# A two-layer decoder trunk on one core: half-size staging tiles, five modulation units on VectorE, their ends spread over steps, running sums seeded by ScalarE

## The chip, the core and the metric

The kernel runs on one core of a Trainium2 chip. The metric is the device time of one execution in microseconds, the median of repeated runs; the profile is one such execution. TensorE (PE, its weight loads shown apart as PEld), VectorE (DVE), ScalarE (ACT), GpSimd (POOL) and the sequencer that issues the weight transfers (SP) work in parallel, each through its own instructions in a fixed order, and wait for each other by semaphores.

## What is computed

Two layers act on x (256 tokens of 2048 features). Layer 0 has MoBA and sliding-window attention, layer 1 forgetting attention and NSA; each is followed by a squared-ReLU MLP with 8192 hidden features. Everything is float32. A vector c modulates every layer, and this modulation is what the change deals with:

```python
cond = jax.nn.silu(c)
for i in range(DEPTH):
    mod = cond @ ada_w[i] + ada_b[i]                 # (2048) @ (2048, 12288)
    sh1, sc1, g1, sh2, sc2, g2 = split(mod, 6)
    h = rms_norm(x, norm_mix_g[i]) * (1.0 + sc1) + sh1
    y = even_mixer(h, ...) if i % 2 == 0 else odd_mixer(h, ...)   # projections, attention, w_out
    x = x + g1 * y
    h = rms_norm(x, norm_mlp_g[i]) * (1.0 + sc2) + sh2
    x = x + g2 * (square(relu(h @ mlp_up[i])) @ mlp_down[i])
return rms_norm(x, final_norm_g)
```

## The kernel before

All weights are streamed once from HBM, some 600 MB. `load` (L299) brings a tile of 512 rows by 512 columns (1 MB, one transfer at L301) into the pool `wst` (four buffers), and splits it for TensorE in two halves of 128x1024: ScalarE writes the rounded part `wh` (L306), VectorE the remainder `wl` (L308). Each product is then three float32r matmuls: wh with the rounded activation, wh with its remainder, wl with the rounded activation. So one full load feeds 48 matmuls of 256 columns, and this step (load, its two conversions, 48 matmuls) is the unit in which the program advances. `kproj` (L361) is a step of a projection whose sums over the input features are made in five groups (the even input projection) or four (half of layer 0's `mlp_up`): after each group the partial sum of a 128x512 tile is kept in SBUF. Of the two tiles of a step, the second (i == 1) is brought back into PSUM by ScalarE ahead of the next group's matmuls (L370, a "seed") and copied out by ScalarE (L390); the first is added by VectorE (L392). `proj` and `down` are steps whose sums stay in PSUM.

The modulation product, 2048 by 12288 for each layer, is cut into units by `ada` (L226). A unit streams its weight columns through the same `wst` pool (L236). With `tensor` set it runs on TensorE (L241): a matmul for each group of 128 input rows into a 32-partition strip of a PSUM bank `row`, four strips at a time. Without it, VectorE multiplies and adds each group of 128 rows into an accumulator `acc` (L245, L248). At its end (L258 to L268) a unit transposes `acc` on TensorE, four transposes to a block of 512 columns, into the one bank `aux`, VectorE reduces the block (L260), and adds the bias. A 1024-column unit has two such blocks, and both use `aux`.

Units wait in a queue. `tick`, called once in a step, adds a rate to a credit and for each whole credit pulls one transfer of the next unit, with the arithmetic that belongs to it; `need` pulls until named units are done. The rates and the tables that say which units run on TensorE stand at the top of the file. Layer 0's (scale, shift) pairs, all of layer 0's gates g1 (four units, all on TensorE), scales sc2 and shifts sh2 (eight units, two on TensorE), gates g2 (four units, one on TensorE), and then layer 1's twelve units of 1024 columns (VectorE) stand in it in this order: 24 units, nine on TensorE.

In order of time the program has these stages: the even input projection and attention; `down` for `even_w_out`; half of layer 0's `mlp_up` in four groups (`up_streamed`, L659); the rest of layer 0's MLP (`mlp`, L523); layer 1's mixer (`odd`); its `down`; layer 1's MLP. Between them stands a norm, in which PE waits for VectorE and ScalarE.

Instructions are issued in an order that the compiler's scheduler makes from the program's; semaphores are set by it too. `causal_head` (L575) scales the probabilities of an attention head; its 256-column part runs on VectorE (L590) with `NORM_A` off.

## Time and profile before

| | |
|---|---|
| median of 3 runs | 2323.24 us (2321.38 to 2324.72) |
| the profiled execution, its own time | 2327.63 us |
| its span, first to last instruction | 2325.8 us |
| mean granted TensorE clock | 0.983 |
| PE busy | 2243.2 us, 96% |
| DVE busy | 1669.5 us, 72% |
| ACT busy | 1114.7 us, 48% |
| HBM read | 594.95 MB, 257 GB/s over the span |

Busy is the time in which an engine has at least one instruction in flight. Matmuls overlap each other, so a row's mean duration of some 280 ns is the latency of one, not its share of the span. The granted clock is that of TensorE, 1.0 being 2.4 GHz and 0.5 being 1.2 GHz. A unit in what follows is a modulation unit.

### The profile page before, as it was taken

What the parts mean: (1) busy time and instruction counts of PE and PEld (TensorE: products, weight loads), DVE (VectorE), ACT (ScalarE), POOL (GpSimd) and SP (SyncE); (2) the same over time, 40 slices, a digit from 0 to 9 for tenths busy, and PEclk for the clock granted to TensorE, in tenths of its full rate; (3) what the DMA queues carried; (4) which work ended last, traced back from release to release, by engine and by line L of the source; (5) the groups of instructions that cost most, each with busy time, mean ns of one, the idle gap of its engine ahead of it and who ended that gap; (6) DMA issues with size and microseconds to landing.
All of it is one profiled execution on the core that took longest, in us unless ns stands there. A gap on an engine that the chain in (4) does not pass through costs nothing.

```text
span 2325.8 us, 44699 instructions
## 1 busy us (share of the span) xinstructions
PE 2243.2 (96%) x18762; PEld 2156.4 (93%) x18762; DVE 1669.5 (72%) x2456; ACT 1114.7 (48%) x1742; POOL 4.6 (0%) x25
## 2 busy tenths in 40 slices
PE   7899999999999999999999999998999999999998
PEld 5799789899999999999999988998999999999998
DVE  3888888797767777787876988888644654655555
ACT  4555753555744344344444555444544543543543
POOL 0000000000000000000000000000000000000000
PEclk9999999999999999999999999999999999999999
DMA  9899688899978778787857877886655656656652
GB/s 308 322 326 357 228 281 319 278 323 316 321 280 290 271 272 305 274 313 267 311 198 244 310 266 245 329 302 230 197 199 188 194 199 190 192 199 192 191 194 95
DMA packets 285819, 599.94 MB, mean 258 GB/s; under 512 B 14290, under 2 KB 23346, under 8 KB 285618
## 3 DMA queue, kind: packets, MB, share of 16 engines
q1 hardware_dynamic: 285072, 596.34, 74.2%
q8 instruction: 147, 2.41, 0.4%
q10 hardware_dynamic: 546, 0.75, 0.1%
q14 instruction: 54, 0.44, 0.1%
HBM read 594.95 MB, written 2.10 MB: 257 GB/s over the span
## 4 chain that ended last, share of the span: by engine, by line
issue 65%; PE 21%; DVE 7%; DMA 5%; ACT 2%; SPq 0%; POOL 0%; POOLq 0%; DVEq 0%; ACTq 0%
PE mm L386 6%; PE mm L320 6%; DMA wa<-in_ada_w_dram 3%; DVE wl L308 3%; DVE acc L248 2%; PE bank L386 1%; PE row L241 1%; PE mm L329 1%; PE mm L330 1%; PE mm L328 1%; DMA w<-in_odd_w_out_dram 1%; PE bank L593 1%; PE bank L556 1%; ACT wh L306 1%; DVE sacc L155 0%
## 5 line engine op out<-in xcount | busy, mean ns | idle before, releaser
L308 DVE TENSOR_TENSOR wl<-w,wh 128x1024 fp32r<-128x1024 f32 x736 | 878.9, 1220 | 415.2 <-ACT wh L306 414.3
L306 ACT ACTIVATE wh<-w 128x1024 fp32r<-128x1024 f32 x736 | 751.6, 1055 | 855.4 <-PE mm L320 673.4
L320 PE MATMUL mm<-hs,wh 128*128 128x256 f32 x5120 | 886.2, 278 | 3.9 <-DVE hs L408 3.0
L320 PEld LDWEIGHTS mm<-hs,wh 128*128 128x128 f32 x5120 | 776.6, 189 | 5.5 <-DVE hs L408 3.2
L320 PE MATMUL mm<-xs,wh 128*128 128x256 f32 (+1 forms) x4128 | 720.4, 279 | 2.4 <-ACT xs L454 2.2
L320 PE MATMUL mm<-hs,wl 128*128 128x256 f32 x2560 | 711.4, 278 | 4.0 <-DVE wl L308 3.8
L320 PEld LDWEIGHTS mm<-xs,wh 128*128 128x128 f32 (+1 forms) x4128 | 627.8, 189 | 5.6 <-ACT xs L454 3.4
L320 PE MATMUL mm<-xs,wl 128*128 128x256 f32 x2064 | 572.8, 279 | 1.7 <-DVE wl L308 1.6
L320 PEld LDWEIGHTS mm<-hs,wl 128*128 128x128 f32 x2560 | 482.8, 189 | 6.3 <-DVE wl L308 6.0
L248 DVE SCALAR_TENSOR_TENSOR acc<-wa,cond,acc 128x1024 f32<-128x1024 f32 (+1 forms) x360 | 389.1, 1081 | 108.3 <-DMA wa<-in_ada_w_dram 104.0
L320 PEld LDWEIGHTS mm<-xs,wl 128*128 128x128 f32 x2064 | 388.2, 188 | 3.3 <-DVE wl L308 2.8
L386 PE MATMUL mm<-xs,wh 128*128 128x256 f32 x1792 | 318.4, 281 | 0.3 <-ACT wh L306 0.3
L386 PEld LDWEIGHTS mm<-xs,wh 128*128 128x128 f32 x1792 | 273.9, 189 | 19.2 <-issue 9.2
L386 PE MATMUL mm<-xs,wl 128*128 128x256 f32 x896 | 249.6, 279 | 3.1 <-DVE wl L308 3.1
L386 PEld LDWEIGHTS mm<-xs,wl 128*128 128x128 f32 x896 | 169.2, 189 | 4.8 <-DVE wl L308 3.7
L390 ACT ACTIVATE u<-mm 128x512 f32<-128x512 f32 x88 | 51.7, 589 | 70.3 <-PE mm L386 69.5
L565 ACT ACTIVATE p<-p,st 128x128 f32<-128x128 f32 (+1 forms) x96 | 40.2, 420 | 29.3 <-DVE st L579 14.7
L536 ACT ACTIVATE t<-mm 128x256 f32<-128x256 f32 x96 | 36.4, 379 | 34.1 <-PE mm L320 24.6
L386 PE MATMUL mm<-wh,xs 128*128 128x256 f32 x256 | 50.0, 290 | 0.9 <-ACT wh L306 0.8
L258 PE MATMUL aux<-cst,acc 128*128 128x128 f32 x192 | 31.5, 285 | 19.6 <-DVE s L260 10.2
L241 PE MATMUL row<-wa,cond 128*32 128x512 f32 x288 | 47.1, 628 | 2.1 <-DMA wa<-in_ada_w_dram 2.1
L151 ACT ACTIVATE t<-xT 128x256 f32<-128x256 f32 x60 | 24.6, 414 | 45.3 <-DVE xT L471 45.3
(214 smaller groups left out, 1458.2 us busy)
## 6 DMA issues: line engine op xcount, KB each, us to landing
wa<-in_ada_w_dram SPq DMA_DIRECT2D x160, 1024.0 KB, 6.2
w<-in_mlp_up_dram SPq DMA_DIRECT2D x128, 1024.0 KB, 5.7
w<-in_mlp_down_dram SPq DMA_DIRECT2D x128, 1024.0 KB, 5.1
w<-in_odd_w_in_dram SPq DMA_DIRECT2D x44, 1024.0 KB, 5.7
wa<-in_ada_w_dram SPq DMA_DIRECT2D x64, 512.0 KB, 5.9
w<-in_even_w_in_dram SPq DMA_DIRECT2D x27, 1024.0 KB, 7.0
w<-in_even_w_out_dram SPq DMA_DIRECT2D x16, 1024.0 KB, 5.3
w<-in_odd_w_out_dram SPq DMA_DIRECT2D x16, 1024.0 KB, 6.5
```

Source lines behind the costliest of these rows:

```text
L151: A.activation(s, xT[:, kt, :], AF.Square)
L241: T.matmul(row[32 * i:32 * i + 32, :], cond[:, k:k + 1].to_broadcast([128, 32]), w[:, i, :], start=t == 0, stop=t == KT // kn - 1, tile_po ...
L248: V.scalar_tensor_tensor(acc, w[:, i, :], cond[:, k:k + 1], acc, op0=ALU.mult, op1=ALU.add)
L258: T.transpose(ps[:, i, :], acc[:, 512 * b + 128 * i:512 * b + 128 * i + 128], ident)
L306: A.activation(wh, w[:, g:g + KS, :], AF.Copy)
L308: V.tensor_tensor(wl, w[:, g:g + KS, :], wh.bitcast(F32), op=ALU.subtract)
L320: T.matmul(P[0:m, 0:S], st[:, c0:c0 + m], mv, start=f and i == 0, stop=e and i == 2)
L328: T.matmul(Ps[j][:, 0:n], hi, wh[:, c0:c0 + n], start=f, stop=False)
L386: T.matmul(Ps[i][:, 256 * h:256 * h + 256], st, mv, start=first and e == 0, stop=last and e == 2, skip_group_check=True)
L390: A.activation(flat[i], P, AF.Copy)
L536: A.activation(r, P[:, 0:S], AF.Relu)
L565: A.activation(p[:, o:o + n], p[:, o:o + n], AF.Exp, bias=m[:, i:i + 1], accum_out=den[:, i:i + 1])
```

## The change

Seven things are changed together.

- `wst` has eight buffers of half the size; `load` issues two transfers of 256 rows by 512 columns instead of one of 512 rows, and a unit's transfer carries half as many rows. `tick` adds twice the rate, so the rows of a unit that go with a step stay as they were at an equal rate.
- Two of the four g1 units, both sh2 units and the g2 unit that ran on TensorE go to VectorE. On VectorE they are joined into 1024-column units: one for the second half of g1, four for (sc2, sh2), two for g2. All of these have 16 transfers, and one multiply-add of 128x1024 goes with each.
- A unit on TensorE takes its four strips in turn over two transfers (two strips for each).
- A unit's end is no longer done at once. `columns` puts its blocks in a queue `late`; a `tick` takes one of them before it pulls, and `need` takes all. The two blocks of a unit use two banks, `aux` and `row`.
- In `kproj` both tiles of a step are seeded and copied out by ScalarE; the addition on VectorE goes.
- `NORM_A` is on. The rate during `down` of `even_w_out` goes from 0.7 to 1.0, and g1 is asked for block by block in that stage rather than ahead of it.
- The compression weights of the odd layer are loaded in halves too.

```diff
-NS = 4
+NS = 8
-R_OUT = 0.7
+R_OUT = 1.0
-NORM_A = False
+NORM_A = True
@@ ada
-            kn = D // cols
+            kn = KS * 512 // cols
...
-                        T.matmul(row[32 * i:32 * i + 32, :], cond[:, k:k + 1].to_broadcast([128, 32]), w[:, i, :], start=t == 0, stop=t == KT // kn - 1,
-                                 tile_position=(0, 32 * i))
+                        q = 32 * (k % 4)
+                        T.matmul(row[q:q + 32, :], cond[:, k:k + 1].to_broadcast([128, 32]), w[:, i, :], start=k < 4, stop=k >= KT - 4,
+                                 tile_position=(0, q))
...
-                    for b in range(n // 4):
-                        ps = aux((128, 4, 128))
...
+                    columns(l, secs, c0, cw, tensor, acc)
...
+        late = deque()
+
+        def columns(l, secs, c0, cw, tensor, acc):
+            red = s32()
+            blocks = cw * len(secs) // 512
+
+            def block(b):
+                ps = psx.tile([128, 4, 128], F32, tag=("aux", "row")[b], name="cps")
+                for i in range(4):
+                    T.transpose(ps[:, i, :], acc[:, 512 * b + 128 * i:512 * b + 128 * i + 128], ident)
+                src = ps.rearrange("p a (j q) -> p a j q", q=32)[:, :, :, 0] if tensor else ps
+                V.tensor_reduce(red[:, 4 * b:4 * b + 4], src, AX.X, ALU.add)
+                if b < blocks - 1:
+                    return
...
+            for b in range(blocks):
+                late.append(lambda b=b: block(b))
@@ tick and need
-            credit[0] += rate[0]
+            if late:
+                late.popleft()()
+            credit[0] += 2 * rate[0]
...
+            while late:
+                late.popleft()()
@@ load
-            w = wst.tile([128, kn, ncol], F32, tag="w", name="w")
-            SP.dma_start(w, W[r0:r0 + 128 * kn, c0:c0 + ncol].rearrange("(k p) n -> p k n", p=128))
             for g in range(0, kn, KS):
+                w = wst.tile([128, KS, ncol], F32, tag="w", name="w")
+                SP.dma_start(w, W[r0 + 128 * g:r0 + 128 * (g + KS), c0:c0 + ncol].rearrange("(k p) n -> p k n", p=128))
...
@@ kproj
-            seeded = [g > 0 and not held and i == 1 for i in range(len(outs))]
+            seeded = g > 0 and not held
...
-                        if g == 0 or held or seeded[i]:
-                            A.activation(flat[i], P, AF.Copy)
-                        else:
-                            V.tensor_tensor(flat[i], P, flat[i], op=ALU.add)
+                        A.activation(flat[i], P, AF.Copy)
@@ the queue of units
+        queue(0, (2,), True, 0, 512)
+        queue(0, (2,), True, 512, 512)
+        queue(0, (2,), False, 1024, 1024)
         for g in range(4):
-            queue(0, (2,), G1_T[g] == "1", 512 * g, 512)
-        for g in range(4):
-            queue(0, (4,), SC2_T[g] == "1", 512 * g, 512)
-            queue(0, (3,), SH2_T[g] == "1", 512 * g, 512)
-        for g in range(4):
-            queue(0, (5,), G2_T[g] == "1", 512 * g, 512)
+            queue(0, (4, 3), False, 512 * g, 512)
+        for c0 in (0, 1024):
+            queue(0, (5,), False, c0, 1024)
```

Two places show what this does to the order of instructions. Rows with an x are repeated instructions; line numbers differ between the two kernels (L258 and L263 are the transposes of a unit's end, L260 and L265 their reductions, L248 and L245 the multiply-adds, L308 and L321 the remainders `wl`).

In `mlp` of layer 0, the TensorE stream of before around the end of a 1024-column unit:

```order
L258 MATMUL aux<-cst,acc 128x128 x4
L320 MATMUL mm<-hs,wh 128x256 x2
L320 MATMUL mm<-hs,wl 128x256
L320 MATMUL mm<-hs,wh 128x256 x2
L320 MATMUL mm<-hs,wl 128x256
L320 MATMUL mm<-hs,wh 128x256 x2
L320 MATMUL mm<-hs,wl 128x256
L320 MATMUL mm<-hs,wh 128x256 x2
L320 MATMUL mm<-hs,wl 128x256
L320 MATMUL mm<-hs,wh 128x256 x2
L320 MATMUL mm<-hs,wl 128x256
L258 MATMUL aux<-cst,acc 128x128 x4
```

The second block's four transposes stand 15 matmuls behind the first's. The same stream of the changed kernel around the first block of such an end:

```order
L333 MATMUL mm<-hs,wh 128x256 x2
L333 MATMUL mm<-hs,wl 128x256
L263 MATMUL cps<-cst,acc 128x128 x4
L333 MATMUL mm<-hs,wh 128x256 x2
L333 MATMUL mm<-hs,wl 128x256
L333 MATMUL mm<-hs,wh 128x256 x2
L333 MATMUL mm<-hs,wl 128x256
```

Here the second block's transposes follow 32 rows (48 matmuls, one step) further on, and they write another bank.

The VectorE stream of before at such an end (`acc` by L245 opens the next unit, `mod` is the finished piece of the modulation):

```order
L245 TENSOR_SCALAR acc<-wa,cond 128x1024
L260 TENSOR_REDUCE s<-aux 128x4
L308 TENSOR_TENSOR wl<-w,wh 128x1024
L260 TENSOR_REDUCE s<-aux 128x4
L308 TENSOR_TENSOR wl<-w,wh 128x1024
L265 TENSOR_TENSOR mod<-s,adab 128x8
```

And of the changed kernel:

```order
L245 SCALAR_TENSOR_TENSOR acc<-wa,cond,acc 128x1024
L321 TENSOR_TENSOR wl<-w,wh 128x1024
L265 TENSOR_REDUCE s<-cps 128x4
L321 TENSOR_TENSOR wl<-w,wh 128x1024
L245 SCALAR_TENSOR_TENSOR acc<-wa,cond,acc 128x1024 x2
L321 TENSOR_TENSOR wl<-w,wh 128x1024
L265 TENSOR_REDUCE s<-cps 128x4
L321 TENSOR_TENSOR wl<-w,wh 128x1024
L272 TENSOR_TENSOR mod<-s,adab 128x8
```

The two reductions had one instruction between them and now have four, multiply-adds of the next unit among them; and that next unit's first `acc` no longer stands ahead of the first reduction.

In the streamed half of `mlp_up`, the ScalarE stream of the changed kernel (L383 is the seed, L402 the copy out, L319 the rounded part `wh`), where before each step had one seed and one copy out:

```order
L402 ACTIVATE u<-mm 128x512
L383 ACTIVATE mm<-u 128x512
L402 ACTIVATE u<-mm 128x512
L319 ACTIVATE wh<-w 128x1024
L383 ACTIVATE mm<-u 128x512
L319 ACTIVATE wh<-w 128x1024
```

These six rows are one step: two copies out, two seeds and two conversions.

## Rows read from the trace of the kernel before

**Rows 1.** The page: busy time by engine, and DMA in 40 slices.
```profile
PE 2243.2 (96%) x18762; PEld 2156.4 (93%) x18762; DVE 1669.5 (72%) x2456; ACT 1114.7 (48%) x1742; POOL 4.6 (0%) x25
...
DMA  9899688899978778787857877886655656656652
```

**Rows 2.** Stretches: us, busy us of each engine (instructions), granted clock, DMA share, GB/s.
```profile
30.00:205.00 175.00, 160.78 (x1297) 154.02 (x1298) 142.81 (x158) 91.46 (x126) 0.00 (x0) 0.95 0.93 328
...
297.00:402.00 105.00, 104.95 (x892) 100.34 (x887) 90.41 (x156) 50.17 (x80) 0.00 (x0) 1.00 0.87 306
402.00:610.00 208.00, 198.20 (x1662) 184.52 (x1661) 161.72 (x230) 125.18 (x190) 0.69 (x1) 0.98 0.90 307
610.00:1173.00 563.00, 544.65 (x4684) 538.96 (x4684) 429.22 (x504) 237.73 (x312) 0.00 (x0) 0.98 0.81 289
...
1740.00:1798.00 58.00, 58.00 (x514) 58.00 (x514) 24.52 (x21) 25.70 (x33) 0.00 (x0) 1.00 0.61 194
```

**Rows 3.** Groups by shape: count, busy us, mean ns, idle before, its releasers.
```profile
L241 PE MATMUL row<-wa,cond 128*32 128x512 f32 x288 | 47.1, 628 | 2.1 <-DMA wa<-in_ada_w_dram 2.1
...
L258 PE MATMUL aux<-cst,acc 128*128 128x128 f32 x192 | 31.5, 285 | 19.6 <-DVE s L260 10.2 <-DVE acc L248 8.1 <-ACT acc L254 1.1
```

**Rows 4.** TensorE's modulation matmuls alone, by stretch: us, PE, PEld, ACT busy, clock, DMA.
```profile
404.00:418.00 14.00, 4.04 (x16) 0.49 (x16) 0.00 (x0) 0.81 0.95 330
...
580.00:616.00 36.00, 4.26 (x32) 0.63 (x32) 0.59 (x1) 1.00 0.90 312
```

**Rows 5.** Order of time at a unit's end: start us, us, engine, operation, idle before.
```profile
840.25 0.28 PE L320 MATMUL mm<-xs,wl 128*128 128x256 f32 x1
843.37 0.75 DVE L245 TENSOR_SCALAR acc<-wa,cond 128x1024 f32<-128x1024 f32 x1 [4.10 <-DMA wa<-in_ada_w_dram]
844.03 0.68 DVE L260 TENSOR_REDUCE s<-aux 128x4 f32<-128x512 f32 x1
...
844.77 1.11 PE L258 MATMUL aux<-cst,acc 128*128 128x128 f32 x4 [4.24 <-DVE s L260]
```

**Rows 6.** Stretches: behind that end, at two norms, and with the most traffic.
```profile
844.00:852.00 8.00, 7.23 (x44) 7.23 (x45) 5.02 (x8) 0.65 (x1) 0.00 (x0) 0.65 0.43 130
404.00:418.00 14.00, 10.26 (x60) 5.96 (x59) 11.17 (x22) 5.12 (x10) 0.69 (x1) 0.81 0.95 330
...
180.00:190.00 10.00, 10.00 (x90) 10.00 (x89) 9.74 (x9) 4.20 (x7) 0.00 (x0) 1.00 1.03 383
```

**Rows 7.** Groups by shape on DVE and ACT.
```profile
L308 DVE TENSOR_TENSOR wl<-w,wh 128x1024 fp32r<-128x1024 f32 x736 | 878.9, 1220 | 415.2 <-ACT wh L306 414.3
L306 ACT ACTIVATE wh<-w 128x1024 fp32r<-128x1024 f32 x736 | 751.6, 1055 | 855.4 <-PE mm L320 673.4 <-PE mm L330 34.2 <-PE mm L386 33.9
...
L248 DVE SCALAR_TENSOR_TENSOR acc<-wa,cond,acc 128x1024 f32<-128x1024 f32 x225 | 288.1, 1280 | 89.5 <-DMA wa<-in_ada_w_dram 87.3
...
L248 DVE SCALAR_TENSOR_TENSOR acc<-wa,cond,acc 128x512 f32<-128x512 f32 x135 | 101.0, 748 | 18.8 <-DMA wa<-in_ada_w_dram 16.7
L390 ACT ACTIVATE u<-mm 128x512 f32<-128x512 f32 x88 | 51.7, 589 | 70.3 <-PE mm L386 69.5
...
L392 DVE TENSOR_TENSOR u<-mm,u 128x512 f32<-128x512 f32 x56 | 38.3, 685 | 8.0 <-PE mm L386 7.9
...
L370 ACT ACTIVATE mm<-u 128x512 f32<-128x512 f32 x56 | 33.3, 595 | 5.8 <-DVE u L392 5.6
...
L471 DVE SCALAR_TENSOR_TENSOR xT<-mm,mod,xT 128x256 f32<-128x256 f32 x64 | 29.3, 478 | 7.4 <-PE mm L320 7.4
...
L155 DVE TENSOR_TENSOR sacc<-sacc,t 128x256 f32<-128x256 f32 x56 | 23.5, 420 | 3.1 <-ACT t L151 1.9
```

**Rows 8.** DMA issues: count, KB each, median us from issue to landing.
```profile
wa<-in_ada_w_dram SPq DMA_DIRECT2D x160, 1024.0 KB, 6.2
...
wa<-in_ada_w_dram SPq DMA_DIRECT2D x64, 512.0 KB, 5.9
```

**Rows 9.** Who waited for whom from 402 to 610 us: total us, times, longest us.
```profile
PE aux L258 <- DVE acc L248: 6.1, 3, 3.9
```

More of the change, by code (lines that the diff above doesn't have):

```diff
@@ L382, in kproj @@
                             tri3 = ((hi, wh[:, c:c + n]), (hi, wl[:, c:c + n]), (lo, wh[:, c:c + n]))
-                        first = h == 0 and k == 0 and not seeded[i] and not (held and g)
+                        first = h == 0 and k == 0 and not seeded and not (held and g)
                         last = h == 1 and k == kn - 1 and (end or not held)
@@ L487, in hst_out, with down @@
             return [[u_tile().rearrange("p a c -> p (a c)") for _ in range(4)] for _ in range(2)]
-        def down(W, row0, tiles, order, ev):
+        def down(W, row0, tiles, order, ev, lazy=None):
             for blk in range(4):
@@ L887, in build @@
         rate[0] = R_OUT
-        need(0, (0, 2))
-        down(even_w_out[0], 0, o, (2, 3, 0, 1), residual(0, 2, True))
+        down(even_w_out[0], 0, o, (2, 3, 0, 1), residual(0, 2, True), (0, 2))
         R = norm_scale(sumsq())
```

47 lines of the change are left out of this document (21 added, 26 removed).

## The prediction, on record before the changed kernel ran

> **What bounds the kernel now.** I read the page's busy times first, then a table of stretches, then the groups by shape, then the order of time where TensorE (PE) stops. PE is busy for 96% of the span, DVE for 72%, ACT for 48% [rows 1]. In the last third nothing disturbs PE: it issues 514 matmuls in 58 us at full clock [rows 2], 0.1128 us each, so a step of 48 matmuls costs 5.41 us. That is the pace to which everything else is compared. In layer 1's MLP, with DVE at 24.5 of 58 us and DMA at 0.61, no part of the change can help or hurt; it is left out. PE is the bound, so two things count: work that leaves PE, and time in which PE stands. The exceptions are the stretches up to 610 us, where a second limit lies close behind: DMA is at 0.87 to 0.93 of its share, DVE at 82% (142.81 of 175 us), 86% (90.41 of 105) and 78% (161.72 of 208) [rows 2].
>
> **Five units leave PE.** All nine units' matmuls together were busy for 47.1 us [rows 3], 5.2 us a unit, but this holds two units at the start, half of them at low clock. A unit in the open, from 580 to 616 us, takes 4.26 us for its 32 instructions [rows 4]; I take 4.3, and 21 us for five (5.2 would give 26). Against this stand two corrections. Sixteen instructions of one unit, 4.04 us, are issued from 404 to 418 us [rows 4], where PE waits for the norm and the clock is at 0.81 [rows 6]: part of it covers idle time, so some 2 us are not gained. And a remaining unit on PE has two strips for each transfer instead of four. Where transfers are not issued next to each other, eight rounds replace four, each about a quarter of 4.26 us, 1.07 us. The order shows this for the second unit only, +4 us, in a stretch in which DMA sets the pace; the two g1 units come in groups of 4 to 9, one round more each. I charge 1 us. Net gain: 18 us (from 15 to 24).
>
> **The ends of units.** The transposes of a unit's end have 19.6 us of PE idle time ahead of them: 10.2 for the reduction of the block before (the one bank), 8.1 for the last multiply-add, 1.1 for ScalarE [rows 3]. The largest shows how it comes about [rows 5]: PE comes to the second block, whose bank waits for the reduction; the reduction stands on DVE behind the next unit's first multiply-add, and this waits 4.10 us for its transfer; PE stands for 4.24 us. In the changed order the first block comes one step after the last pull, 5.41 us later in PE's time than now, which is more than the longest of these waits, and the second block has a bank of its own. So a wait of either kind needs a DVE that is over 5.4 us late. Only the three 1024-column units ahead of attention still end at once, with some 2 us of the 19.6. Gain: 17 us. Then there is the clock: from 844 to 852 us it is at 0.65, so behind the 4.24 us gap 70% of 8 us ran at 1.2 GHz [rows 6], which loses 2.8 us. The stretches from 402 to 1173 us have a mean of 0.98 [rows 2]: 2% of 771 us, 15 us lost. Some of it belongs to norms and other waits, which stay. I give a third to the ends, two such losses: 6 us. Gain: 23 us together (from 14 to 28; the low end where half of the waits only move). The transposes themselves, 192 in number, stay.
>
> **Work that comes to DVE, and work that leaves it.** The additions go: 56 x 0.685 = 38.3 us; so does the scaling of 24 heads, which I leave out of the sum. The multiply-adds change from 225 of 1.280 and 135 of 0.748 us [rows 7] to 330 of 1.280 (22 units, 15 each; their first products are cheaper and alike), plus 33 us; five reductions of full blocks add 3 us. In all DVE has some 2 us less, so it is no new bound over the whole. It is by stretch: up to 205 us it loses 24 additions, 16 us of its 142.81; during `down` of `even_w_out` it gains. There a step has two `wl` of 1.220, and a quarter of four residual updates with their squares, 0.478 + 0.420 [rows 7]: 3.34 us. To this the old rate adds 0.7 x 4 x 0.748 = 2.09 us, and the new one 1.0 x 2 x 1.280 = 2.56. So 5.43 becomes 5.90 us, against PE's 5.41: DVE is 0.49 us over for 16 steps, 8 us. These durations overlap a little, since the same stretch shows DVE busy for 86% only, which speaks for less. In the streamed half of `mlp_up` DVE would lose 24 additions (16 us) and gain the accumulation of two sh2 units, and comes out some 7 us higher by the changed order's count, at 168 us, with PE needing some 185.
>
> **DMA in the same stretches.** From 402 to 610 us, 307 GB/s x 208 us are 64 MB. PE without three of its units (13 us) and without the stops at ends (8 us with their clock) would want the stretch in 187 us, or 341 GB/s. From 180 to 190 us the trace shows 383 [rows 6], but the mean from 30 to 205 us, where PE waits for data, is 328 at a share of 0.93 [rows 2]. So DMA can take part of the gain. For DVE and DMA together I give back 8 us (from 0 to 18: nothing if DMA holds 341, and 18 if the stretch from 402 keeps 328 and thus lasts 195 us, 8 more, beside DVE's 8 and 2 for the order).
>
> **Half-size tiles.** The pool holds the same bytes, but a half is freed as soon as it is converted, and the 512 KB loads of the first two groups no longer take a whole 1 MB buffer. What this is worth no row shows. Up to 205 us PE is busy for 160.78 of 175 us, so at most 14 us are to be had, and by DMA, from 328 to at most 383 GB/s, more; with DVE 16 us lighter there I take a gain of 4 us (from -6, a loss, to 12). What speaks against smaller transfers is that 512 KB land in 5.9 us and 1024 KB in 6.2 [rows 8]: a transfer hardly gets faster by being smaller. But eight in flight at 5.9 us would be 711 GB/s, far above what moves, so this latency stays hidden. The Trainium skill, in DMA: Bandwidth & Descriptors (section Bandwidth), has the rule against this: batch transfers to at least 1 MiB for 75% of peak. Its table gives 341 GB/s for 1 MB, and by the fit in its section on the anatomy of one DMA (2.0 us and 436 GB/s) an estimate for 512 KB is 164 GB/s one at a time. By that alone the stages up to 610 us would take twice as long; the trace's landing times agree with a large fixed part, but its 383 GB/s at 1 MB show that transfers overlap.
>
> **ScalarE's seeds.** ACT gets 56 seeds of 0.595 and 56 copies out of 0.589 us, 66 us. A step of `mlp_up` then has on ACT two copies out, two seeds and two `wh` of 1.055 [rows 7]: 4.48 us, under 5.41. Four PSUM banks serve two steps, so while PE works on one step ACT empties and seeds the pair of the other, 2.37 us plus conversions in between. I cost this at nothing; what hides it is PE's 5.41 us. In the second group, with steps of 24 matmuls, PE takes 2.7 us and ACT 2.37 + 1.06 = 3.4: eight steps, 6 us over, where DMA sets the pace of some 4.5 us a step. So the bounds are 0 and 6.
>
> **The sum.** 18 + 23 + 4 - 8 - 0 = 37 us less. The profiled execution took 2327.6 us (span 2325.8), 4.4 above the median of 2323.2; I subtract from the median: 2286 us.
>
> **Rivals.** (a) *The freed PE time is taken by DVE and DMA up to 610 us.* There the five units (18) come to nothing, and so do the ends in the stretch from 402 us, 6.1 us of idle time [rows 9] and 2 of clock. Of 23 + 4 some 19 are left, less 2 at the start: 17, or 2306 us. For it: DVE at 5.90 against 5.41, DMA at 0.90. Against it: busy shares of 78% and 86%. (b) *ACT becomes the gate of the seeded steps.* The first matmul of a step now waits for both seeds, and they stand in ACT's order behind the copies out of two steps ago. If the bank comes late by one copy and one seed, 1.18 us, in each of 56 steps, 66 us are lost: 2286 + 66 = 2352 us. It decides from 0.66 us a step (37 / 56). For it: ACT already waits 69.5 us for PE at L390 [rows 7]; against it: 4.48 us of work in 5.41. (c) *Smaller transfers are slower.* If the rate up to 610 us falls by a tenth where DMA is at 0.9, that is some 8% of 580 us, 46 us: 2332 us. For it: the landing times [rows 8]. It rests on the rows; the skill's rule on batching points the same way. (d) *The ends are not cured,* because DVE is late by more than a step: only half of 23 us, and 2297.
>
> **Chances and range.** My forecast with its own spread, (d) included, 0.68; (a) 0.18; (b) 0.06; (c) 0.05; something within the noise of no change, 0.03. Bounds of the terms: most favourable 24 + 28 + 12 - 0 = 64, or 2259; least favourable 15 + 14 - 6 - 18 - 6 = -1, or 2324. All of them at one end is unlikely, so I cut to 2263 and 2313, which takes in (a) and (d) and leaves out (b) and (c). 0.2% (4.6 us) is about what a measurement of this kernel can tell from no change: faster by more 0.84 (0.67 of the forecast and 0.17 of (a)), within it 0.06, slower 0.10 ((b) and most of (c)).
>
> **What would show it.** Right: PE busy with the modulation units for some 20 to 27 us instead of 47.1, transposes of ends with under 4 us of idle time, a granted clock of 0.99 from 610 us on, `mlp` of layer 0 some 13 us shorter, and DVE over 90% busy in `down` of `even_w_out`. Wrong: PE idle ahead of L399 matmuls with the seed L383 as releaser (b), a DMA rate under 300 GB/s with its share at 0.9 up to 600 us (c), transposes that still wait for DVE (d), or `wl` as the releaser of PE in the first 600 us (a).

## The result and the profile after

The changed kernel took 2293.26 us (median of 4 runs, 2290.15 to 2296.93), the kernel before 2323.98 us beside it (median of 4, 2321.38 to 2328.48). The ratio is 0.9858, with a 95% interval from 0.983 to 0.9885: 31 us or 1.4% faster. The profiled execution took 2290.15 us. Forecast were 2286 us, in a range from 2263 to 2313.

The forecast for the whole came out; several of its terms did not, and most of what follows is about that. The page of the changed kernel, first its span, busy times and the DMA slices (compare [rows 1]):

```profile
span 2288.4 us, 45838 instructions
...
PE 2216.7 (97%) x18602; PEld 2147.1 (94%) x18602; DVE 1662.1 (73%) x2341; ACT 1180.4 (52%) x1873; POOL 5.6 (0%) x25
...
DMA  9999679999998988988858876985555656555652
```

TensorE is busy for 26.5 us less, VectorE for 7 us less, ScalarE for 66 us more. The stretches of the changed kernel (us, busy us of each engine with instructions, granted clock, DMA share, GB/s), to be held against [rows 2]: the first 205 us, `down` of `even_w_out`, the streamed half of `mlp_up`, the rest of layer 0's MLP, and the eight microseconds that [rows 6] showed at 1.2 GHz for the greater part:

```profile
30.00:205.00 175.00, 160.34 (x1254) 149.41 (x1253) 130.25 (x137) 114.09 (x169) 0.00 (x0) 0.94 0.93 330
305.00:412.00 107.00, 104.85 (x880) 101.99 (x879) 105.24 (x159) 53.97 (x95) 0.00 (x0) 1.00 0.91 325
422.00:601.00 179.00, 179.00 (x1563) 179.00 (x1564) 160.24 (x181) 140.97 (x221) 0.00 (x0) 0.99 0.96 340
601.00:1138.00 537.00, 532.81 (x4667) 531.14 (x4666) 425.89 (x488) 241.27 (x321) 0.00 (x0) 1.00 0.89 302
844.00:852.00 8.00, 8.00 (x73) 8.00 (x72) 6.95 (x12) 6.10 (x12) 0.00 (x0) 1.00 0.95 342
```

In the streamed half TensorE now never stands (179.00 of 179 us, at a clock of 0.99), and in the rest of the MLP it stands for 4.2 us, at 1.00. Before, it stood for 18.4 of 563 us in the rest of the MLP, at 0.98, and for 6.1 us in the streamed half, which without its norm is this stretch:

```profile
417.00:617.00 200.00, 193.94 (x1650) 183.27 (x1647) 156.62 (x220) 124.77 (x189) 0.00 (x0) 0.99 0.89 305
```

VectorE is 98% busy in `down` of `even_w_out` (105.24 of 107 us), and the first 205 us move at the same 330 GB/s and the same share as before. By groups (count, busy us, mean ns, idle before and its releasers; [rows 3] and [rows 7] before):

```profile
L238 PE MATMUL row<-wa,cond 128*32 128x512 f32 x128 | 29.3, 654 | 1.9 <-DVE s L265 0.9 <-DMA wa<-in_ada_w_dram 0.8
L263 PE MATMUL cps<-cst,acc 128*128 128x128 f32 x192 | 29.0, 275 | 0.7 <-ACT acc L249 0.7
L245 DVE SCALAR_TENSOR_TENSOR acc<-wa,cond,acc 128x1024 f32<-128x1024 f32 x330 | 423.1, 1282 | 98.1 <-DMA wa<-in_ada_w_dram 96.3
L402 ACT ACTIVATE u<-mm 128x512 f32<-128x512 f32 x144 | 84.1, 592 | 73.9 <-PE mm L399 73.0
L383 ACT ACTIVATE mm<-u 128x512 f32<-128x512 f32 x112 | 65.5, 597 | 1.2
```

The units' matmuls went from 47.1 us for nine units to 29.3 us for four, and the 19.6 us of idle time ahead of the ends' transposes to 0.7. For a seed (L383) TensorE waited once, for 1.3 us.

To place the time I cut each profile at the same TensorE matmuls: the first and last of a group of the projection, of `down`, and so on. The stages in us, worked out from the two traces; the two norms of layer 1 are left out. The first matmuls of a `down` lie between the last ones of attention, so the cut between these two is loose: by the first matmul of `down` of `even_w_out` that stage takes 101.6 us after instead of 96.7, and attention's as much less. Sums over both do not depend on it.

| stage | before | after | difference |
|---|---|---|---|
| start | 27.0 | 26.8 | -0.2 |
| even input projection, first group | 32.5 | 37.0 | +4.5 |
| its other groups, and attention | 249.4 | 248.3 | -1.1 |
| `down` of `even_w_out` | 95.2 | 96.7 | +1.5 |
| norm | 10.4 | 10.3 | -0.1 |
| streamed half of `mlp_up` | 200.0 | 179.3 | -20.7 |
| rest of layer 0's MLP | 561.3 | 537.5 | -23.8 |
| odd mixer | 315.1 | 320.9 | +5.8 |
| `down` of `odd_w_out` | 103.7 | 101.2 | -2.5 |
| layer 1's MLP | 717.7 | 717.2 | -0.5 |

The gain sits in two stages, 44.5 us, and some 7 us of it are given back, on balance, ahead of them and behind them. These are differences of two single executions, whose spans lie 37.4 us apart, where the medians lie 31 apart: a few us of a stage can be the executions' own.

What stands behind the 23.8 us is seen in the waits. In the rest of layer 0's MLP before (617 to 1178 us; who waited for whom, us in total, times, longest):

```profile
DVE acc L248 <- DMA wa<-in_ada_w_dram: 85.1, 37, 5.7
...
PE aux L258 <- DVE s L260: 8.7, 4, 4.2
...
PE mm L320 <- DVE wl L308: 5.4, 11, 1.0
...
PE mm L320 <- DVE hs L408: 3.0, 1, 3.0
```

And after, from 601 to 1138 us:

```profile
DVE acc L245 <- DMA wa<-in_ada_w_dram: 69.9, 61, 3.7
DVE wl L321 <- ACT wh L319: 34.1, 30, 3.0
...
PE mm L333 <- DVE wl L321: 3.7, 4, 3.2
```

VectorE still waits 70 us for the modulation's transfers, but in 61 pieces instead of 37 and never for more than 3.7 us. In the order of time (start us, us, engine, operation, idle before) two such waits after a step, where [rows 5] had one of 4.10 us with TensorE behind it:

```profile
838.36 1.28 DVE L245 SCALAR_TENSOR_TENSOR acc<-wa,cond,acc 128x1024 f32<-128x1024 f32 x1 [1.02 <-DMA wa<-in_ada_w_dram]
...
839.56 2.35 DVE L321 TENSOR_TENSOR wl<-w,wh 128x1024 fp32r<-128x1024 f32 x2
...
842.92 1.29 DVE L245 SCALAR_TENSOR_TENSOR acc<-wa,cond,acc 128x1024 f32<-128x1024 f32 x1 [1.01 <-DMA wa<-in_ada_w_dram]
```

TensorE issues without a break through both.

### The profile page after: what moved, and what is told of

Its sections match the earlier page's. It is cut to its first block, busy times and chain, and to the rows that moved or that the text cites. A ratio compares the mean times of both kernels' runs of the same rounds, so it can differ in the third digit from the quotient of the medians.

```text
span 2288.4 us, 45838 instructions
## 1 busy us (share of the span) xinstructions
PE 2216.7 (97%) x18602; PEld 2147.1 (94%) x18602; DVE 1662.1 (73%) x2341; ACT 1180.4 (52%) x1873; POOL 5.6 (0%) x25
## 4 chain that ended last, share of the span: by engine, by line
PE 47%; issue 33%; DVE 8%; DMA 7%; ACT 4%; SPq 0%; DVEq 0%; POOLq 0%; POOL 0%; ACTq 0%
PE mm L333 30%; PE mm L399 12%; DMA wa<-in_ada_w_dram 5%; DVE wl L321 3%; DVE acc L245 2%; PE bank L399 1%; ACT wh L319 1%; DMA w<-in_odd_w_in_dram 1%; PE row L238 1%; DMA w<-in_even_w_in_dram 1%; PE cps L263 1%; ACT u L402 1%; ACT mm L383 0%; PE bank L605 0%; ACT hs L417 0%
## 5 line engine op out<-in xcount | busy, mean ns | idle before, releaser
L321 DVE TENSOR_TENSOR wl<-w,wh 128x1024 fp32r<-128x1024 f32 x736 | 881.6, 1221 | 421.3 <-ACT wh L319 417.2
L319 ACT ACTIVATE wh<-w 128x1024 fp32r<-128x1024 f32 x736 | 754.1, 1055 | 771.4 <-PE mm L333 666.6
L245 DVE SCALAR_TENSOR_TENSOR acc<-wa,cond,acc 128x1024 f32<-128x1024 f32 x330 | 423.1, 1282 | 98.1 <-DMA wa<-in_ada_w_dram 96.3
L402 ACT ACTIVATE u<-mm 128x512 f32<-128x512 f32 x144 | 84.1, 592 | 73.9 <-PE mm L399 73.0
L383 ACT ACTIVATE mm<-u 128x512 f32<-128x512 f32 x112 | 65.5, 597 | 1.2
L343 PE MATMUL mm<-wh,xs 128*128 128x256 f32 (+1 forms) x128 | 43.7, 342 | 0.0
```

Of the source, the lines that this page charges most:

```text
L245: V.scalar_tensor_tensor(acc, w[:, i, :], cond[:, k:k + 1], acc, op0=ALU.mult, op1=ALU.add)
L319: A.activation(wh, w, AF.Copy)
L321: V.tensor_tensor(wl, w, wh.bitcast(F32), op=ALU.subtract)
L343: T.matmul(Ps[j][:, 0:n], lo, wh[:, c0:c0 + n], start=False, stop=e)
L383: A.activation(P, flat[i], AF.Copy)
L402: A.activation(flat[i], P, AF.Copy)
```

## The experiments

Two theories were open. The prediction's: ends that come a step later in two banks remove TensorE's waits, and units that leave TensorE are worth their matmul time. Against it: the transfers' size does it, by cutting the waits in VectorE's order, and late ends are beside the point. The first four kernels undo one part of the change, the next three do one part alone or vary the pool, then come the norm flag and the rate, and two kernels that try to mend what the change lost. Ratios are to the kernel before, run beside each; its medians there are 2330 to 2331 us, and the changed kernel itself gave 0.9858 [0.983, 0.9885] and, run again, 0.9864 [0.984, 0.9888]. A ratio can differ from the quotient of the medians by 0.002 (0.9842 for that second run), so differences of under 5 us between kernels of different comparisons are not told apart. Stage times are each from one execution. TensorE's rows of an experiment stand at other lines than after's, by a few.

### Undo: ends at once

The two banks stay; a unit's blocks are done as soon as its last pull is.

```diff
                     columns(l, secs, c0, cw, tensor, acc)
+                    while late:
+                        late.popleft()()
```

> The changed kernel, but a unit's blocks are taken at once again when its last multiply-add is issued; the two banks stay. My theory, that spreading the ends over steps is what shortened layer 0's MLP by 24 us (560.8 to 536.9 us) and part of the streamed half of mlp_up (200.2 to 179.4): some 15 to 23 us of it come back, time about 2308 to 2316 us, and the transposes have some 10 us or more of idle time ahead of them again. Rival, that the half-size tiles did it by bringing weights earlier: under 6 us come back, below 2299 us. If the second bank alone was the cure, only the waits for the multiply-adds return (8 us before): about 2301 us.

Measured: 2289.14 us, ratio 0.982 [0.9792, 0.9848]. That is not slower than with late ends. Its transposes, and its rest of layer 0's MLP:

```profile
L265 PE MATMUL cps<-cst,acc 128*128 128x128 f32 x192 | 26.0, 273 | 2.3 <-DVE acc L245 1.6 <-ACT acc L249 0.7
```

```profile
600.00:1137.00 537.00, 532.70 (x4675) 531.71 (x4674) 428.85 (x490) 245.29 (x328) 0.00 (x0) 1.00 0.90 306
```

Only 1.6 us more of waiting come back, out of 19, and the stage takes 536.7 us as after. With small transfers and a bank for each block, lateness has nothing left to cure. The theory that late ends made this gain falls.

### Undo: full tiles

`wst` has four buffers of 1 MB again, and each load and unit pull is one transfer of 1 MB (the compression weights of the odd layer too); all else as in the changed kernel.

```diff
-NS = 8
+NS = 4
-            kn = KS * 512 // cols
+            kn = D // cols
-            credit[0] += 2 * rate[0]
+            credit[0] += rate[0]
...
+            w = wst.tile([128, kn, ncol], F32, tag="w", name="w")
+            SP.dma_start(w, W[r0:r0 + 128 * kn, c0:c0 + ncol].rearrange("(k p) n -> p k n", p=128))
             for g in range(0, kn, KS):
-                w = wst.tile([128, KS, ncol], F32, tag="w", name="w")
-                SP.dma_start(w, W[r0 + 128 * g:r0 + 128 * (g + KS), c0:c0 + ncol].rearrange("(k p) n -> p k n", p=128))
```

> The changed kernel with full-size tiles again (four buffers, one transfer of 512 rows, units with twice the rows in a transfer, rates single); everything else stays changed. My theory, that the half-size tiles give nothing and cost some 4 us at the start, where a TensorE unit runs in twice as many rounds: 2286 to 2292 us, with the first 70 us some 4 us shorter, and layer 0's MLP unchanged. Rival, that the tiles bring the data earlier and so keep DVE from being late: 2300 us or more, with the MLP of layer 0 longer by 8 us or more.

Measured: 2307.47 us, 0.9898 [0.9863, 0.9933]. Against the changed kernel's 2293 to 2294 that is some 13 us slower by medians and 8 to 9 by ratios, whose intervals overlap a little. The streamed half takes 183.2 us instead of 179.3, and the rest of the MLP 554.3 instead of 537.5. Windows of these two, and the waits of the second:

```profile
423.00:606.00 183.00, 181.07 (x1563) 180.28 (x1564) 160.84 (x182) 136.76 (x219) 0.00 (x0) 0.98 0.95 334
...
606.00:1161.00 555.00, 540.18 (x4673) 536.17 (x4671) 430.40 (x493) 243.36 (x323) 0.00 (x0) 0.99 0.84 295
```

```profile
DVE acc L245 <- DMA wa<-in_ada_w_dram: 69.0, 34, 6.5
...
PE mm L333 <- DVE wl L321: 9.5, 14, 1.9
```

VectorE waits the same 69 us for transfers as with small ones, but in 34 pieces of up to 6.5 us, and TensorE then stands for 14.8 us (555 less 540.18) instead of 4.2. Its ends are late and have two banks all the while. So the size of the pieces is what counts in layer 0's MLP. The finer order on VectorE comes with the smaller transfers, and no run parts the two.

### Undo: half of the seeds

The first tile of a step is added by VectorE again.

```diff
-            seeded = g > 0 and not held
+            seeded = [g > 0 and not held and i == 1 for i in range(len(outs))]
...
-                        A.activation(flat[i], P, AF.Copy)
+                        if g == 0 or held or seeded[i]:
+                            A.activation(flat[i], P, AF.Copy)
+                        else:
+                            V.tensor_tensor(flat[i], P, flat[i], op=ALU.add)
```

> The changed kernel with the additions of the first tile of a step back on VectorE (56 of 0.685 us). My theory, that in the streamed half of mlp_up DVE is now close to a bound, so that taking 24 additions from it was needed to cash the units that left TensorE: that stage gets 6 to 14 us longer, the even projection 0 to 4, time 2299 to 2311 us. Rival, that seeds on ScalarE make no difference, or cost what they save, since DVE had idle time there: within 4 us of 2293.

Measured: 2297.97 us, 0.9863 [0.9839, 0.9887]; the streamed half takes 179.9 us. By medians 4 us slower than the changed kernel, by ratios equal: no difference that can be told. The 66 us more that ScalarE has to do in the changed kernel gain nothing that can be measured here, and cost nothing.

### Undo: units back on TensorE

Nine units on TensorE, cut as before, with the shifts due as before; g1 is still asked for block by block in `down`, and half tiles, late ends and the rest stay. The edit of the due times is left out here.

```diff
...
-        queue(0, (2,), True, 0, 512)
-        queue(0, (2,), True, 512, 512)
-        queue(0, (2,), False, 1024, 1024)
-            queue(0, (4, 3), False, 512 * g, 512)
-        for c0 in (0, 1024):
-            queue(0, (5,), False, c0, 1024)
+            queue(0, (2,), True, 512 * g, 512)
+        for g in range(4):
+            queue(0, (4,), False, 512 * g, 512)
+            queue(0, (3,), g % 2 == 1, 512 * g, 512)
+        for g in range(4):
+            queue(0, (5,), g == 1, 512 * g, 512)
```

> The changed kernel with nine units on TensorE as before, and the others of layer 0 in 512 columns again; ends spread, tiles half, seeds all on ScalarE. My forecast gave the five units 18 us: 2311 us. The stage times now say that the two g1 units brought nothing up to the end of down (412.1 us against 407.5 before), so that three units in the streamed half of mlp_up are all: 8 to 13 us, 2301 to 2306. If DVE and DMA limits took even that: below 2298.

Measured: 2306.12 us, 0.9899 [0.9876, 0.9922], 12 us slower than the changed kernel by medians and 8 to 10 by ratios. The streamed half, and TensorE's modulation matmuls in it and ahead of it (PE, PEld, ACT):

```profile
424.00:617.00 193.00, 191.11 (x1611) 181.01 (x1612) 148.40 (x206) 144.76 (x227) 0.00 (x0) 0.98 0.94 322
```

```profile
398.00:422.00 24.00, 5.29 (x32) 0.76 (x32) 0.12 (x1) 1.00 0.99 353
426.50:619.20 192.70, 10.59 (x64) 1.51 (x64) 1.20 (x2) 0.98 0.94 322
```

It takes 192.6 us against 179.3 and, in the second run of the changed kernel, 180.4. Two of the five units ran there (64 of their records, 32 a unit). They kept TensorE busy for 10.6 us, 5.3 us a unit and not the 4.26 of [rows 4], because with half tiles a unit runs in more and thinner rounds (shown further down). Of the 12 to 13 us that the stage is longer, these are the greater part. So what left TensorE there was gained whole, although VectorE in the changed kernel is busy 12 us longer in the stage for it. The other three units, two of g1 and the first of sh2 (398 to 422 us), ran ahead of it: the stages from the first group to the end of `down` took 389.7 us against 382.0 and 384.9, 5 to 8 us more. The rest of layer 0's MLP did not change (536.6).

### Alone: half tiles

The kernel before with half-size buffers, loads and pulls only (the edit of the full tiles the other way round). A unit on TensorE then takes its strips over two transfers, as in the change, and there are nine of them.

> The kernel before with half-size staging tiles alone (eight buffers, halved transfers, rate doubled; ends at once through one bank, nine units on TensorE, additions on VectorE). Theory formed after the first four runs: TensorE waited at a unit's end because VectorE was late, and VectorE was late because it stood in its order behind a transfer that came late; half-size tiles let that transfer be issued earlier, so they alone shorten layer 0's MLP from 561 to 537 to 547 us, and the streamed half of mlp_up by some 6 us: time 2296 to 2310 us against 2324 to 2330 of before, and the waits of transposes for multiply-adds go from 8 to under 3 us. Rival, that the second bank or the later step is needed for it: MLP of layer 0 stays at 555 us or more, time within 6 us of before.

Measured: 2326.03 us, 0.9982 [0.9962, 1.0002]: no difference that can be told. Inside it is not the same kernel. Its rest of layer 0's MLP takes 544.1 us instead of 561.3, while its transposes wait nearly as long as before, for the one bank:

```profile
613.00:1157.00 544.00, 534.41 (x4666) 530.08 (x4665) 425.99 (x503) 240.93 (x319) 0.00 (x0) 1.00 0.88 300
```

```profile
L259 PE MATMUL aux<-cst,acc 128*128 128x128 f32 x192 | 31.4, 287 | 18.3 <-DVE s L261 13.9 <-DVE acc L249 3.4 <-ACT acc L255 0.7
```

The waits for the last multiply-add fell from 8.1 to 3.4 us; those for the bank did not (13.9 against 10.2). So 17 of the 24 us in this stage come with the small transfers alone. They are given back elsewhere: 12 us from the first group to the end of `down` (389.1 us against 377.1) and 11.5 in the odd mixer (326.6 against 315.1). For the first of these there is a candidate, TensorE's modulation matmuls in that stretch, before and here:

```profile
29.90:407.20 377.30, 25.86 (x160) 4.07 (x160) 2.98 (x5) 0.98 0.86 305
```

```profile
29.15:418.40 389.25, 36.70 (x160) 5.56 (x160) 2.99 (x5) 0.98 0.87 300
```

The same 160 records are busy for 10.8 us more, the thinner rounds again. So this run is not small transfers alone, and it does not show what they would give with full rounds. Its profiled execution took 2333.43 us, 7 above the run's median, which belongs to the stages' losses too.

### Alone: ends

The kernel before with the new `columns`, the queue `late` and the two banks only (as in the diff of the change).

> The kernel before with the spread ends alone (two banks, one block taken in a tick), tiles and all else as before. My prediction: 17 us of waits and 6 us of low clock go, 2301 us where before is 2324. Theory after the first four runs: transposes no longer wait, but VectorE is as late as before, so that TensorE waits for its remainders wl or activations instead: layer 0's MLP 552 to 556 us instead of 561, time 5 to 12 us less than before.

Measured: 2325.73 us, 0.9973 [0.9952, 0.9995], some 6 us of gain (1 to 11 by the interval), against 23 forecast. In the stage in which the ends were to help most, 564.2 us against 561.3, the profiled execution (2331.35 us, 6 above the run's median) shows no gain at all. Its window and waits:

```profile
616.00:1180.00 564.00, 543.84 (x4672) 536.08 (x4665) 428.42 (x504) 236.65 (x311) 0.00 (x0) 0.99 0.82 288
```

```profile
DVE acc L248 <- DMA wa<-in_ada_w_dram: 94.4, 36, 6.1
...
PE mm L336 <- DVE wl L324: 15.1, 28, 1.7
```

The transposes hardly wait any more (2.2 us), yet TensorE stands for 20.2 us, more than before: its matmuls wait 28 times for `wl`. VectorE's waits for transfers are as long as ever (up to 6.1 us), and what is queued behind them is now the remainder of the next load instead of a reduction. The wait changed its name. This is the prediction's rival (d), a VectorE that is late by more than a step, and its place is the kernel with 1 MB transfers.

### Six buffers instead of eight

```diff
-NS = 8
+NS = 6
```

Is it the size of a transfer, or the number of buffers that small ones allow? With six, the pool holds 3 MB instead of 4.

> The changed kernel with six staging buffers of half size instead of eight (3 MB instead of 4 MB in the pool). If what the half-size tiles give is data that arrives earlier, then less room makes transfers late again: layer 0's MLP back to 545 us or more from 537, time 2300 to 2320 us. If the gain lies in the smaller pieces themselves (finer interleaving on DMA and on the engines), six are as good as eight: within 4 us of 2293.

Measured: 2314.34 us, 0.9918 [0.9886, 0.9949]. The rest of layer 0's MLP takes 539.8 us, nearly as with eight, and its waits for transfers are as short (63 of at most 3.0 us):

```profile
DVE acc L245 <- DMA wa<-in_ada_w_dram: 79.9, 63, 3.0
```

So there it is the size of the pieces and not their number. The 20 us are lost in other stages, 12 to 14 of them in `down` of `even_w_out` (111.1 us against 96.7 and 98.6). Its window, and what ScalarE waited for in it:

```profile
310.00:425.00 115.00, 105.62 (x845) 101.65 (x844) 100.42 (x141) 49.39 (x79) 0.00 (x0) 0.96 0.90 306
```

```profile
ACT wh L319 <- DMA w<-in_even_w_out_dram: 27.1, 14, 6.1
```

With eight buffers ScalarE waits for no weights worth a row in this stage. So the size of a transfer counted in the one stage, and the number of buffers in the other, where weights came late.

### The norm flag

```diff
-NORM_A = True
+NORM_A = False
```

> The changed kernel with the scaling of attention heads back on VectorE (24 instructions of 347 ns, 16 of them in the even layer and 8 in the odd). The odd mixer became 5.6 us longer by the change (315.1 to 320.9 us). If ScalarE's scaling, behind others in its order, holds up the heads there: 3 us or more of it come back, and the even heads gain likewise, 2288 to 2291 us. If not: odd mixer within 1.5 us of 320.9, time within 3 us of 2293.

Measured: 2297.57 us (two runs), 0.9847 [0.9811, 0.9883]. Not told apart from the changed kernel. Attention's group and `down` together take 197.5 us with the flag off, against 189.8 and 191.4 with it on; but a version below with the flag on (strip pairs) takes 196.1, so this does not show that the flag helps. The odd mixer, slower after by 5.8 us, stays at 319.7 and does not owe its time to it.

### The rate

The prediction priced the higher rate during `down` of `even_w_out` as a cost.

```diff
-R_OUT = 1.0
+R_OUT = 0.7
```

> The changed kernel with the rate during down of even_w_out back at 0.7 instead of 1.0 pulls a step. My prediction had a step there at 5.90 us on VectorE against 5.41 on TensorE, and gave back 8 us to it. If so, down and attention together get 3 to 8 us shorter; but about 5 pulls of 1 MB move into later stages, which now stand at 5.6 us a step on TensorE with VectorE at some 83%: streamed mlp_up 0 to 3 longer. Time 2288 to 2296 us. If the rate of 1.0 is right, because these pulls would else press into the streamed mlp_up: 2 us or more longer.

Measured: 2326.98 us, 0.999 [0.9978, 1.0001]: the whole gain is gone, 33 us against the changed kernel's 2294.33 beside it. The streamed half takes 212.5 us instead of 180. From 412 to 640 us TensorE waits for the activations `xs`:

```profile
PE mm L399 <- ACT xs L464: 24.0, 4, 9.4
```

The longest of the four, in order of time (L265 is the last reduction of a (scale, shift) unit, L272 its `mod`, L463 and L464 make the activations from it):

```profile
587.79 1.28 DVE L245 SCALAR_TENSOR_TENSOR acc<-wa,cond,acc 128x1024 f32<-128x1024 f32 x1 [1.29 <-DMA wa<-in_ada_w_dram]
...
591.32 1.28 DVE L265 TENSOR_REDUCE s<-cps 128x4 f32<-128x512 f32 x2
...
593.80 0.15 DVE L272 TENSOR_TENSOR mod<-s,adab 128x4 f32<-128x4 f32 x1
...
595.11 1.27 DVE L463 SCALAR_TENSOR_TENSOR t<-xT,mod,sacc 128x256 f32<-128x256 f32 x3
...
595.62 1.30 ACT L464 ACTIVATE xs<-t,mod 128x256 fp32r<-128x256 f32 x3 [7.21 <-DVE t L463]
...
596.18 1.23 PE L399 MATMUL mm<-xs,wh 128*128 128x256 f32 x4 [9.43 <-ACT xs L464]
```

```profile
586.00:600.00 14.00, 4.57 (x25) 4.33 (x24) 12.29 (x21) 4.22 (x8) 0.00 (x0) 0.71 0.88 310
```

The group's modulation is finished only when the group is due: TensorE stands for 9.4 of these 14 us, and the granted clock of the stretch is 0.71, a mixture of both levels. The four waits are 24.0 of the 32 us that the stage is longer; the granted clock from 412 to 640 us was 0.93, against 0.97 from 412 to 601 us of the changed kernel, which is likely part of the rest. The changed kernel asks for g1 only inside `down`, so those pulls come out of the same rate; 0.7 leaves the (scale, shift) units too far behind, and 1.0 has them done ahead of their groups.

### The changed kernel again, and two versions of it

The changed kernel, unaltered, beside the next two.

> The changed kernel once more, beside the two attempts at a better one: 2290 to 2300 us, stage times within 1.5 us of the first profile.

Measured: 2294.33 us (2291.74 to 2302.73), 0.9864 [0.984, 0.9888].

The change had lost 4.5 us in the first group. The reason stands in the rounds of the one unit that runs on TensorE there. A round of before had four matmuls on four strips, one of after, with half a transfer's rows, two on two strips; each matmul is two records. First after, then before (start us, us, engine, operation):

```profile
43.30 1.05 PE L238 MATMUL row<-wa,cond 128*32 128x512 f32 x4
```

```profile
41.49 1.06 PE L241 MATMUL row<-wa,cond 128*32 128x512 f32 x8
```

Four matmuls take 1.06 us and two take 1.05, so a unit whose rounds are all half-filled takes twice its time. Over all four units that stay on TensorE the changed kernel needs 29.3 us; with full tiles it is 21.2:

```profile
L238 PE MATMUL row<-wa,cond 128*32 128x512 f32 x128 | 21.2, 628 | 3.5 <-DMA wa<-in_ada_w_dram 2.2 <-DVE s L265 0.9 <-ACT acc L249 0.3
```

One version holds the first transfer back and issues the matmuls of two together:

```diff
+                two.append(w)
+                if tensor and t % 2 == 0:
+                    yield False
+                    continue
-                for i in range(kn):
-                    k = kn * t + i
+                for i in range(kn * len(two)):
+                    k = kn * (t + 1 - len(two)) + i
+                    w = two[i // kn]
...
+                two.clear()
```

> The changed kernel with a TensorE unit's matmuls issued for two transfers together, so that its four strips are again next to each other. The first 37 us step of the even projection took 4.5 us longer by the change (32.5 to 37.0 us from its first matmul to the next group's), and full tiles brought 3.5 of it back. If the thinner rounds are the cause: 3 to 4.5 us less there. If data decides how long the whole even projection lasts, as its sum of 377 against 382 us to the end of down suggests, the gain is gone by the end of down, and the time the same as that of the changed kernel within 3 us; else 3 to 4 us less.

Measured: 2289.89 us, 0.983 [0.9815, 0.9845]. In the first group the unit's rounds are whole again, all but one, and the group takes 34.6 us instead of 37.0 and 37.1:

```profile
43.38 1.06 PE L244 MATMUL row<-wa,cond 128*32 128x512 f32 x8
```

By the end of `down`, though, the sum of the stages is 385.5 us, no better than 382.0 and 384.9. In the other units the rounds stay mixed, and the units' matmuls are busy for 29.2 us in all, as before this edit. So the loss in the first group was real, but by the end of `down` nothing of it is seen. All four times (2286.49 to 2290.40) lie below all four of the changed kernel beside it (2291.74 to 2302.73), so some gain of the whole is likely; no stage shows where.

The other adds to this that the units of the first (scale, shift) pairs end at once, as in the first experiment:

```diff
                     columns(l, secs, c0, cw, tensor, acc)
+                    while late and secs == (1, 0):
+                        late.popleft()()
```

> The same with the ends of layer 0's (scale, shift) units done at once, through two banks. With all ends at once the second and third group of the even projection took 108.1 us together instead of 114.6, and attention and down after them 200.3 instead of 189.8. If the early ends are the gain and the late ends of g1 belong to attention: 5 us less than the kernel with strip pairs. If both follow from how the scheduler fills a stage that data limits, the sum to the end of down stays at 378 to 388 us and the time is the same within 4 us.

Measured: 2287.64 us, 0.9828 [0.9809, 0.9848], and 380.4 us to the end of `down`. It is the fastest kernel of the study by its median, 6.7 us below the changed kernel in the same comparison, but the intervals of the two ratios overlap, and so does the kernel with all ends at once (0.982). That these versions beat the changed kernel by some 0.3% is likely and not settled.

## Why the prediction was right, and where its steps were wrong

The time of 2293 us lies 7 us above the forecast and well inside the range. That the sum came so near is in part luck: the largest term, 23 us for the ends, is worth nothing by the runs, and the term of 4 us for the tiles is worth two to three times as much. Undone one at a time, units and tiles give some 16 to 25 of the 31 us, and no single edit accounts for the rest. Step by step:

**The bound.** Right. TensorE was the bound and DVE and DMA lay close behind it only up to 610 us; layer 1's MLP changed by 0.5 us.

**Five units, 18 us.** Right in kind: 12 us by the medians of the undo (2306.1 against 2294.3), 15 to 16 by the spans (2304.7 against 2288.4 and 2290.0), 8 to 10 by the ratios. But the undo prices units in thin rounds, which keep TensorE busy for 5.3 us each in the streamed half; the prediction's 4.3 is for full ones, and what five of those would have cost no run shows. By the records of the kernel before, 10.75 us of units' matmuls and 6.1 us of waits at ends leave the streamed half, 16.8 of its 20.7 us. Ahead of it the undo costs 5 to 8 us for three units, but the change as a whole gained nothing there: 382.0 us from the first group to the end of `down`, against 377.1. Thin rounds were priced too low as work: the prediction counted some 6 us and charged 1; measured are 8.1 us more busy time (29.3 against 21.2 with full tiles), which also puts the units' 29.3 us outside the 20 to 27 that were to show. What they cost in time stays open: the first group lost 4.5 us, and the version that mends it gains nothing by the end of `down`. The prediction's reason, that DMA sets the pace there, fits this and is not shown.

**Ends, 23 us.** Wrong as a term, though the rows that were to show it came true: 0.7 us idle ahead of the transposes, a clock of 1.00 from 601 us. In layer 0's MLP the gain was even what waits and clock together had been priced at, and nearly twice the 13 us that were to show there: 14.2 us less standing and, by difference, 9.6 us in the clock and the rest. But undoing the lateness cost nothing, and doing it alone left that stage as it was. The step that failed is "a wait of either kind needs a DVE that is over 5.4 us late". With 1 MB transfers VectorE is that late or nearly (waits up to 6.1 us, and its arithmetic behind them), and then `wl` is late as well. The prediction looked at the instruction that waited last and not at the other work behind the same VectorE wait.

**Half-size tiles, 4 us, in the first 205 us.** Wrong in size and place. The first 205 us moved 330 GB/s as against 328, at the same share. By undoing, the tiles' gain is 8 to 13 us, most of it where the prediction did not look for one: in layer 0's MLP (554.3 us against 537.5), where VectorE's waits come in smaller pieces and TensorE waits behind them 4 times instead of 14. That its lead covers the pieces is the reading that fits. It is the same kind of VectorE wait, 4.10 us in [rows 5], that the prediction put down to the ends. The bank plays a part too: with small tiles and one bank transposes still waited 18.3 us, with two banks and early ends 2.3. Late ends with a single bank were not tried.

**Give-back, 8 us.** The count of VectorE in `down` was right as a load (98% busy). As a cost it is not seen: the stage grew by 1.5 us, or by 6.4 if it is cut at its first matmul, with attention's stage shorter by as much. Missing was what the rate buys. The rate was priced by its work on VectorE in its own stage, and not by what is due behind it: with 0.7 the streamed half waits for its modulation, and 33 us go. DMA held 340 GB/s at a share of 0.96 in the streamed half, the 341 that the prediction asked for.

**Seeds, 0 us.** Right: 179.00 of 179 us in the stage that ScalarE was to gate, and an undo that is not told from none.

**Not foreseen:** the odd mixer's 5.8 us (3.3 together with its `down`, so that the loose cut does not count). Half of the 5.8 goes with the small tiles (317.8 us with full ones, 326.6 with small ones alone). TensorE waits longer there for VectorE's share of the heads, before (whole span) and after (1144 to 1467 us):

```profile
L817 PE MATMUL bank<-cst,p 128*128 128x128 f32 x24 | 5.3, 295 | 1.3 <-DVE p L812 1.3
```

```profile
L832 PE MATMUL bank<-cst,p 128*128 128x128 f32 x24 | 5.5, 299 | 4.0 <-DVE p L827 4.0
```

That is 2.7 us more for one line. Why small tiles make VectorE late in this stage stays open.

**Rivals.** (a), freed time eaten by limits other than TensorE up to 610 us, fell in the streamed half, where TensorE never stood; ahead of it, up to 412 us, the change as a whole gained nothing, as (a) has it, but which limit took it is not shown, and its sign, `wl` as TensorE's releaser in the first 600 us, stands there for 2.9 us only. (b), ScalarE as the gate, and (c), slower small transfers, fell by the rows above. (d) is true of the ends alone with 1 MB transfers, and hidden in the whole by the tiles.

One count in the text ahead of the prediction is to be set right: the kernel before has 33 units, 24 on VectorE and nine on TensorE (360 multiply-adds of 15 a unit, 288 matmul records of 32 a unit).

## What to carry to other kernels

When an engine with a fixed order serves two streams, and one of them waits for transfers, try smaller pieces for that stream: the sum of the waits may stay (70 us here), but each is shorter, and less of it reaches the next engine. Look then at what else becomes smaller with them, as the rounds on TensorE did here. Moving the one instruction that is seen to wait only hands the wait to the next one in the same order; look at everything that is queued behind the wait. And price a rate of background work by when its products are due, not only by the load it puts on its stage.

## What the runs showed of the hardware

**Smaller transfers were no slower.** The issues of the changed kernel (count, KB each, median us from issue to landing; [rows 8] before):

```profile
wa<-in_ada_w_dram SPq DMA_DIRECT2D x256, 512.0 KB, 5.2
w<-in_mlp_up_dram SPq DMA_DIRECT2D x256, 512.0 KB, 4.4
...
wa<-in_ada_w_dram SPq DMA_DIRECT2D x256, 256.0 KB, 5.1
```

Halving a unit's transfer from 1 MB took its landing from 6.2 to 5.2 us, and a 256 KB one took 5.1. With several in flight the landing hardly followed the size. The streamed half moved 340 GB/s at a share of 0.96 in 512 KB pieces, and 334 at 0.95 in 1 MB pieces, with TensorE as the bound in both. The Trainium skill, in DMA: Bandwidth & Descriptors (section Bandwidth), asks for batches of at least 1 MiB; the rates here, with several transfers in flight, show no loss at half of that.

**A round on two strips took as long as one on four.** Two float32 matmuls on two 32-partition strips took 1.05 us, four on four strips 1.06 us.

**ScalarE's two directions cost alike.** A 128x512 copy out of PSUM took 592 ns and a seed into PSUM 597 ns.
